# A stretch of constant products on TensorE ahead of the first conditioning product

## The chip, the cores and the metric

The kernel runs on one core of one Trainium2 chip. The metric is the time on the device of one execution, in microseconds (us). The profile is of one execution, taken by the hardware profiler. TensorE appears in it twice: PE is the multiplications, PEld the loads of the stationary operand. DVE is VectorE, ACT is ScalarE, POOL is GpSimd, SP is the engine that issues most transfers.

## What is computed

One step of a one-layer decoder for 256 prompt tokens and 32 sample tokens (8 requests of 4), 288 columns in all, in fp32. Cut to what matters here:

```python
mod = (silu(c) @ w_ada + b_ada)            # conditioning: 9 rows (1 prompt, 8 samples) x 2048 -> 6 x 2048
h = rms(x, g_mix) * (1 + sc_m) + sh_m
proj = h @ w_in                            # 2048 -> 9216: gates, convolution input, u, v, merge gates
...                                        # short convolution, spatial gating, merge
x = x + gt_m * (merged @ w_out)
h2 = rms(x, g_ffn) * (1 + sc_f) + sh_f
x = x + gt_f * ((silu(gate) * up) @ w_ffn_out)   # gate, up = split(h2 @ w_ffn_in)
```

The results are the normalised prompt and sample rows, a new convolution state and normalised rows of v.

## The kernel before, in words

All activations lie transposed: features on the 128 partitions, the 288 tokens along the free dimension. A weight tile is 128x128. It is split into a high and a low part in the format fp32r (ACT casts the high part, line L471; DVE subtracts it, L258 and L478), and `triple` multiplies high by high, high by low and low by high into one PSUM bank: three full-array products, 128x288, lines L239, L242 and L244 (or L241). These are called main products below.

The conditioning product is written another way. `Ada.run` (line L403 of the kernel before) takes as stationary operand `cs`, 32 columns (9 in use) of silu(c), and sends 64, 192 or 512 columns of fp32 weights past it, in four column groups of the array, one for each quarter of a bank:

```python
PE.matmul(acc[32 * j : 32 * j + 32, :w], cs[:, kt, :], self.raw[:, o : o + w],
          ..., tile_position=(0, 32 * j), skip_group_check=True)
```

These products come in visits between main products: a visit is a row of them for j = 0, 1, 2, 3 and several kt. The trace shows two records for each such fp32 product.

TensorE's order is the order in which the code issues, since only that engine is scheduled by hand throughout. The program starts with `warm(19)`, 19 bf16 products of a constant tile `wb` into the bank `idle` (L595), then the first conditioning block `a0[0]`, five more warm products, `a0[1]` with six warm products in its middle, `first_tile` (which makes the first operands, and has eight warm products beside it), and the first main products, stream `w0`:

```python
steps = [Do(lambda: warm(19)), a0[0], Do(lambda: warm(5)), a0[1]]
steps += [Do(first_tile), Do(lambda: warm(6))]
```

Weights arrive from HBM through a ring of seven buffers of 128x2048 fp32 (the tag `raw`, `RAW = 7`), issued by SP in program order: `a0` (2 buffers), `w0`, `a1` (2), `wK`, then the blocks of `wA`. A transfer waits until the ring's buffer is free. PSUM has four banks with the tag `main`, of which `idle` is the first one given out.

Of the kernel before, what the change touches and what calls it, by code (L numbers as in the profile page):

```python
# [8 lines left out]
F32 = mybir.dt.float32  # L9
F32R = mybir.dt.float32r  # L10
# [4 lines left out]
P = 128  # L15
D = 2048
T = 288
# [10 lines left out]
RAW = 7  # L28
# [60 lines left out]
def decoder_kernel(tc, d):  # L89
    nc = tc.nc  # L90
    from contextlib import ExitStack

    with ExitStack() as es:
        def pool(name, bufs=1, **kw):
            return es.enter_context(tc.tile_pool(name=name, bufs=bufs, **kw))

        pc = pool("const")
        pw = pool("wstream")
        pslot = pool("slots", MAIN)
        pkept = pool("kept", KEPT)  # L100
        ptmp = pool("tmp", 5)
        pps = pool("psum", 4, space=bass.MemoryType.PSUM)
        with tc.manual_schedule(engines={nc.tensor.engine}):
            _body(tc, nc, d, pc, pw, pslot, pkept, ptmp, pps)


def _body(tc, nc, d, pc, pw, pslot, pkept, ptmp, pps):
    ids = [0]

    def nm(s):  # L110
        ids[0] += 1
        return f"{s}_{ids[0]}"

    def const(name, shape, dt=F32):
        return pc.tile(shape, dt, tag=name, name=name)
# [12 lines left out]
    def psmain():  # L128
        return pps.tile([P, 512], F32, tag="main", name=nm("pm"), bufs=4)
# [4 lines left out]
    V, A, G, PE, SY = nc.vector, nc.scalar, nc.gpsimd, nc.tensor, nc.sync  # L134
# [26 lines left out]
    cs = const("cs", [P, 16, 32])  # L161
# [205 lines left out]
    class Step:  # L367
        defer = False
        raw = None
# [218 lines left out]
    wb = const("wb", [P, 288], BF16)  # L588
    G.memset(wb, 1.0)
    idle = psmain()  # L590
# [498 lines left out]
        tail.close()  # L1089


    rh1 = h1.__getitem__
    def at(main, plan):
        out, n = [], 0
        for s in main:
            out.append(s)
            if isinstance(s, Blk):
                n += 1
                out += plan.pop(n, [])
        assert not plan  # L1100
        return out
# [71 lines left out]
    n = len(steps)  # L1173
    stream = [s for s in steps if not isinstance(s, Do)]
    pos = {id(s): i for i, s in enumerate(stream)}
    order = list(stream)
# [27 lines left out]
    for s in steps:  # L1204
# [11 lines left out]
        i = pos[id(s)]  # L1216
# [124 lines left out]
```

## Time and profile before

| | |
|---|---|
| time, median of 2 runs | 1594.12 us (1593.86 to 1594.39) |
| profiled execution: its own time | 1594.02 us |
| profiled execution: span of the core | 1592.2 us |
| PE busy | 1582.0 us (99%), 12636 records |
| PEld busy | 1518.1 us (95%) |
| DVE busy, ACT busy | 1016.4 us (64%), 735.9 us (46%) |
| granted TensorE clock, mean | 0.998 |

The span is the profile's stretch from the first to the last instruction; the time of the same execution is 1.8 us longer. The record of a product lasts longer than its step, since products overlap: a step is read from one start to the next.

### The profile page before, as it was taken

How to read it: one execution, taken by the hardware profiler on the slowest of the kernel's cores; microseconds unless marked ns; L12 is line 12 of the kernel's file. 1: busy time of each engine (PE TensorE's matmuls, PEld its weight loads, DVE VectorE, ACT ScalarE, POOL GpSimd, SP SyncE). 2: the span in 40 equal slices, each digit the busy share in tenths (PEclk: the TensorE clock that was granted, in tenths of full speed). 3: DMA queues.
4: the chain of work that ended last, by engine and by line, in shares of the span. 5: the costliest groups of instructions: out<-in, count | busy, mean ns of one | idle time of the engine just before them, and what ended most of it. 6: DMA issues, size and time to landing. Idle time of an engine off the chain costs nothing.

```text
span 1592.2 us, 31593 instructions
## 1 busy us (share of the span) xinstructions
PE 1582.0 (99%) x12636; PEld 1518.1 (95%) x12636; DVE 1016.4 (64%) x2200; ACT 735.9 (46%) x1366; POOL 21.4 (1%) x65
## 2 busy tenths in 40 slices
PE   9999999999999999999999999999999999999997
PEld 8998999998998998999998999999999999999997
DVE  6676788877755667667844555555555555555565
ACT  6633344643444434456643444444444444444464
POOL 0000000000000000011000000000000000000000
PEclk9999999999999999999999999999999999999999
DMA  9887866777778666654766556453564534645341
GB/s 382 332 324 282 324 241 219 282 281 304 287 290 340 270 262 229 250 179 167 271 267 226 216 184 212 160 176 112 168 234 159 173 122 164 229 160 174 113 165 60
DMA packets 59476, 357.88 MB, mean 225 GB/s; under 512 B 6720, under 2 KB 10176, under 8 KB 28608
## 3 DMA queue, kind: packets, MB, share of 16 engines
q1 hardware_dynamic: 59040, 355.73, 60.9%
q8 instruction: 99, 1.62, 0.4%
q14 instruction: 49, 0.40, 0.1%
q10 hardware_dynamic: 288, 0.13, 0.0%
HBM read 352.74 MB, written 3.09 MB: 223 GB/s over the span
## 4 chain that ended last, share of the span: by engine, by line
PE 98%; DMA 1%; DVE 1%; issue 0%; DVEq 0%; ACT 0%; ACTq 0%
PE pm L239 31%; PE pm L244 30%; PE pm L242 30%; PE ada L403 5%; DMA raw<-in_wK 1%; DMA raw<-in_w 0%; DVE st L1070 0%; DMA t<-in_c 0%; DVE q L611 0%; PE px L242 0%; PE px L239 0%; PE px L244 0%; PE px L213 0%; PE px L902 0%; PE px L901 0%; PE px L848 0%
## 5 line engine op out<-in xcount | busy, mean ns | idle before, releaser
L239 PE MATMUL pm<-s,hi 128*128 128x288 f32 (+1 forms) x3750 | 1095.3, 292 | 0.0
L242 PE MATMUL pm<-s,hi 128*128 128x288 f32 (+1 forms) x3750 | 1090.6, 291 | 0.0
L244 PE MATMUL pm<-s,lo 128*128 128x288 f32 (+1 forms) x3738 | 1088.1, 291 | 0.0
L471 ACT CAST hi<-raw 128x512 fp32r<-128x512 f32 (+1 forms) x963 | 585.6, 610 | 770.5 <-PE pm L242 739.1
L478 DVE TENSOR_TENSOR lo<-raw,hi 128x512 fp32r<-128x512 f32 (+1 forms) x849 | 578.8, 683 | 417.8 <-ACT hi L471 405.3
L239 PEld LDWEIGHTS pm<-s,hi 128*128 128x128 f32 x3750 | 702.2, 187 | 15.2 <-issue 12.1
L242 PEld LDWEIGHTS pm<-s,hi 128*128 128x128 f32 x3750 | 702.2, 187 | 0.1
L244 PEld LDWEIGHTS pm<-s,lo 128*128 128x128 f32 x3738 | 699.9, 187 | 0.0
L258 DVE TENSOR_TENSOR lo<-raw,hi 128x512 fp32r<-128x512 f32 x111 | 74.5, 675 | 28.4 <-ACT hi L471 27.6
L403 PE MATMUL ada<-raw,cs 128*32 128x512 f32 (+2 forms) x1152 | 88.2, 453 | 0.0
L403 PEld LDWEIGHTS ada<-raw,cs 128*32 128x32 f32 x1152 | 31.1, 110 | 44.5 <-issue 41.4
L793 DVE TENSOR_TENSOR s<-pm,s 128x288 f32<-128x288 f32 x72 | 32.8, 456 | 18.9 <-PE pm L244 18.6
L311 ACT CAST s<-t 128x288 fp32r<-128x288 f32 (+1 forms) x76 | 32.9, 433 | 19.4 <-DVE t L825 12.5
L313 DVE TENSOR_TENSOR s<-t,s 128x288 fp32r<-128x288 f32 (+1 forms) x76 | 35.0, 461 | 6.5 <-ACT s L311 5.7
L353 DVE SCALAR_TENSOR_TENSOR x<-pm,mod,x 128x256 f32<-128x256 f32 x79 | 37.6, 476 | 0.0
L991 DVE SCALAR_TENSOR_TENSOR t<-t,pm 128x288 f32<-128x288 f32 x42 | 19.1, 455 | 19.6 <-PE pm L244 19.6
L785 DVE TENSOR_TENSOR s<-pm,s 128x288 f32<-128x288 f32 x48 | 21.7, 453 | 9.9 <-PE pm L244 9.2
L352 DVE TENSOR_TENSOR t<-pm,mod 128x32 f32<-128x32 f32 x79 | 15.2, 192 | 16.4 <-PE pm L244 15.9
L776 DVE TENSOR_TENSOR s<-s,rb 128x288 f32<-128x288 f32 x48 | 21.6, 449 | 0.0
L181 ACT ACTIVATE t<-x 128x288 f32<-128x288 f32 x29 | 12.9, 444 | 17.4 <-DVE x L356 17.4
L186 DVE TENSOR_TENSOR acc<-acc,t 128x288 f32<-128x288 f32 x33 | 15.0, 455 | 8.2 <-ACT t L181 8.2
L770 DVE SCALAR_TENSOR_TENSOR s<-pm,s 128x256 f32<-128x256 f32 x36 | 17.3, 481 | 2.7 <-PE pm L244 2.7
(168 smaller groups left out, 478.0 us busy)
## 6 DMA issues: line engine op xcount, KB each, us to landing
raw<-in_fi SPq DMA_DIRECT2D x84, 1024.0 KB, 4.8
raw<-in_a SPq DMA_DIRECT2D x64, 1024.0 KB, 7.3
raw<-in_f SPq DMA_DIRECT2D x64, 704.0 KB, 4.0
raw<-in_wD SPq DMA_DIRECT2D x34, 1024.0 KB, 6.3
raw<-in_aE SPq DMA_DIRECT2D x16, 1024.0 KB, 9.7
raw<-in_wo SPq DMA_DIRECT2D x16, 1024.0 KB, 6.0
raw<-in_wC SPq DMA_DIRECT2D x19, 768.0 KB, 4.2
raw<-in_pa SPq DMA_DIRECT2D x8, 1024.0 KB, 6.4
```

The costliest lines, as they stand in the source:

```text
L239: PE.matmul(out, wh, ah, start=first, stop=False)
L242: end_ = PE.matmul(out, wh, al, start=False, stop=turn and last)
L244: end_ = PE.matmul(out, wl, ah, start=False, stop=last)
L258: lows.pop(0)[1]()
L311: A.copy(hi, a)
L313: V.tensor_tensor(lo, a, hi.bitcast(F32), ALU.subtract)
L353: V.scalar_tensor_tensor(x[:, m, :TP], ps[:, :TP], mod[:, gt0 + m, 0:1], x[:, m, :TP], ALU.mult, ALU.add)
L403: PE.matmul(acc[32 * j : 32 * j + 32, :w], cs[:, kt, :], self.raw[:, o : o + w], start=kt == 0, stop=kt == 15, tile_position=(0, 32 * j), ...
L471: A.copy(hi, self.raw[:, s * 128 : e * 128])
L478: sub()
L785: return V.tensor_tensor(part[m], ps[:, :T], part[m], ALU.add)
L793: V.tensor_tensor(a, ps[:, :T], a, ALU.add)
```

## The change

Before everything that PE does in the program, a function `bench` is called. It fills four tiles of the ring `raw`: `f` (fp32, 0.75) and `r0`, `r1`, `r2` (the same in fp32r). PE then multiplies: 48 bf16 products, 30 main-like products, and 24 kinds of visits. A kind is four times nine main-like products, a product at the border ahead of it (or none), 16 column-group products, a product at the border behind it (or none); and nine main-like products at its end. Twelve kinds vary what stands behind, nine what stands ahead, two the order of the column groups, one the width. Nothing reads the results; they go to the bank `idle` and to the three other banks of the tag `main`.

```diff
+    def bench():
+        f = pw.tile([P, 2048], F32, tag="raw", name=nm("bench"), bufs=RAW)
+        V.memset(f, 0.75)
+        rs = []
+        for i in range(3):
+            r = pw.tile([P, 2048], F32R, tag="raw", name=nm("benchr"), bufs=RAW)
+            A.copy(r, f) if i else V.tensor_copy(r, f)
+            rs.append(r)
+        r0, r1, r2 = rs
+        outs = [idle] + [psmain() for _ in range(3)]
+
+        def main(n):
+            for i in range(n):
+                o = 7 if i % 3 == 0 else 519 if i % 3 == 1 else 7
+                r = r1 if i % 3 == 2 else r0
+                PE.matmul(outs[0][:, :T], r[:, P * (i % 8) : P * (i % 8) + P], r2[:, o : o + T], start=True, stop=True)
+
+        def sets(n, w=512, order=(0, 1, 2, 3)):
+            for i in range(n):
+                for j in order:
+                    PE.matmul(
+                        outs[1][32 * j : 32 * j + 32, :w],
+                        cs[:, i % 16, :],
+                        f[:, 512 * j : 512 * j + w],
+                        start=True,
+                        stop=True,
+                        tile_position=(0, 32 * j),
+                        skip_group_check=True,
+                    )
+
+        def bf(n, m=P, times=1):
+            def g():
+                for _ in range(times):
+                    PE.matmul(outs[2][:m, :n], wb[:, :m], wb[:, :n], start=True, stop=True)
+
+            return g
+
+        def fr(n, m=P):
+            return lambda: PE.matmul(outs[2][:m, :n], r0[:, :m], r2[:, 7 : 7 + n], start=True, stop=True)
+
+        def nat(n, m=P):
+            return lambda: PE.matmul(outs[2][:m, :n], f[:, :m], f[:, :n], start=True, stop=True)
+
+        def none():
+            pass
+
+        def visit(before, after, **k):
+            for _ in range(4):
+                main(9)
+                before()
+                sets(4, **k)
+                after()
+            main(9)
+
+        for i in range(48):
+            PE.matmul(idle[:, :T], wb[:, :P], wb, start=True, stop=True)
+        main(30)
+        for after in (none, bf(2), bf(64), bf(128), bf(T), bf(2, P, 2), bf(2, 32), bf(2, 64), fr(2), fr(64), nat(2), fr(2, 64)):
+            visit(none, after)
+        for before in (bf(2), bf(64), bf(2, 32), bf(2, 64), bf(T), fr(2), fr(2, 32), nat(2, 32), nat(2)):
+            visit(before, none)
+        visit(none, none, order=(3, 2, 1, 0))
+        visit(none, none, order=(0, 2, 1, 3))
+        visit(none, none, w=256)
+
+    bench()
```

A call such as `bf(2, 64)` is a bf16 product of 2 columns with a stationary operand of 64 columns; `fr` is the same in fp32r, `nat` in fp32; without a second number the stationary operand has 128 columns. `bf(2, P, 2)` is two of them.

PE before, around the first conditioning block, which is a0[0] (32 products of 64 columns):

```order
L595 LDWEIGHTS wb
L595 MATMUL pm_100<-wb 128x288
L403 MATMUL ada_163<-raw_103,cs 32x64 x32
L595 LDWEIGHTS wb
L595 MATMUL pm_100<-wb 128x288
```

PE now, at the first border product, in the second kind of visit (`benchr_103` is r0, `benchr_105` is r1, `benchr_107` is r2, `bench_101` is f):

```order
L1107 MATMUL pm_100<-benchr_107,benchr_103 128x288 x2
L1107 MATMUL pm_100<-benchr_107,benchr_105 128x288
L1112 MATMUL pm_109<-bench_101,cs 32x512 x16
L1125 LDWEIGHTS wb
L1125 MATMUL pm_110<-wb 128x2
L1107 MATMUL pm_100<-benchr_107,benchr_103 128x288 x2
L1107 MATMUL pm_100<-benchr_107,benchr_105 128x288
```

PE now reaches its first row of before, the 19 warm products of L595, after 1068 new rows; all that followed them before follows them still.

ACT now, from its start; before, the row behind the ACTIVATE was the cast of w0's first weights (L471):

```order
L138 DMA t_75<-in_c 128x144
L140 DMA cp_77<-in_cpack 128x112
L164 ACT_TABLE_LOAD
L164 ACTIVATE t_87<-t_75 128x144
L1098 CAST benchr_105<-bench_101 128x2048
L1098 CAST benchr_107<-bench_101 128x2048
L471 CAST hi_3033<-raw_2898 128x512
```

Two casts of 2048 columns came in ahead of that cast. On DVE the fill of f and the cast of r0 came in ahead of the two instructions that make cs.

SP now, with what each row waits for; `raw_2904` is a1's first buffer, and the rows and their order are those of before, in which that transfer waited for no engine:

```order
L452 DMA raw_2898<-in_w 128x512 [waits DMAHW2_49]
L385 DMA raw_2904<-in_a 128x1024 [waits DVE_49,DMAHW3_49,PE_49,Activation_49]
L385 DMA raw_2904<-in_a 128x1024 [waits DMAHW4_49]
L385 DMA raw_2907<-in_a 128x1024 [waits DMAHW5_49,PE_49]
L385 DMA raw_2907<-in_a 128x1024 [waits DMAHW6_49]
L155 DMA x<-in_x 128x288 [waits DMAHW7_49]
L454 DMA raw_2911<-in_wK 128x768 [waits DMAHW0_49,PE_49]
```

Since the four tiles of bench take the first four buffers of the ring, a1 and wK now wait for PE to be done with f, r0 and r2, and all later transfers stand behind them.

## The prediction

> **What bounds the kernel now.** I read the head of the page, then the chain of work that ended last, the waits of PE, and the order of time on PE where the new products stand.
>
> ```profile
> span 1592.2 us, 31593 instructions
> PE 1582.0 (99%) x12636; PEld 1518.1 (95%) x12636; DVE 1016.4 (64%) x2200; ACT 735.9 (46%) x1366; POOL 21.4 (1%) x65
> PE 98%; DMA 1%; DVE 1%; issue 0%; DVEq 0%; ACT 0%; ACTq 0%
> ```
>
> PE is busy for 99% of the span and carries 98% of the chain. No other engine is near. Whatever is put on PE is therefore added to the span, save where PE would have stood still or done filler work. PE's only such stretch at the place of the change is the start:
>
> ```profile
> 1.13 4.74 PE L595 MATMUL pm<-wb 128*128 128x288 bf16 x19 [1.13 <-POOL wb L589]
> 5.80 1.24 PE L403 MATMUL ada<-raw,cs 128*32 128x64 f32 x64
> 6.97 0.79 PE L595 MATMUL pm<-wb 128*128 128x288 bf16 x5
> 8.28 0.91 PE L595 MATMUL pm<-wb 128*128 128x288 bf16 x6
> 9.12 0.30 PE L403 MATMUL ada<-raw,cs 128*32 128x64 f32 x5
> ```
>
> The first conditioning block starts at 5.80 us. So I reckon one number, the time at which that block starts in the changed program, and shift all behind it by the difference.
>
> **The start of the new stretch.** The rows also give the price of a bf16 product. The first 19 take 4.74 us, about 0.24 each; six later ones take 0.91 of which the last one's record is 0.29, so 0.91 - 0.29 = 0.62 for five steps, 0.124 each. The slow pace lasts until about 5.9 us: the block at 5.80 still needs 1.24 us where the same 64 records take 1.12 to 1.16 later. The Trainium skill, "TensorE: Matmul & The Clock Gate", section "What's actually happening", says that the clock is at half until one window of about 3.4 us was busy; the two paces in the trace agree with the two rates, though here the slow one lasted some 4.8 us. By 3.4 us the sum below would be about 0.7 us smaller.
>
> The 48 new bf16 products start at 1.13 like the old ones: 20 slow ones to 5.9, then 28 x 0.124 = 3.5, so the main-like products can start at 9.4 us. Their operands must be there by then:
>
> ```profile
> 1.08 0.48 DVE L162 MEMSET cs<- 128x512 f32 x1
> 4.69 0.32 ACT L164 ACTIVATE t<-t 128x144 f32<-128x144 f32 x1 [1.75 <-DMA t<-in_c]
> L471 ACT CAST hi<-raw 128x512 fp32r<-128x512 f32 x892 | 549.8, 618 | 708.0 <-PE pm L242 681.2 <-DMA raw<-in_fi 5.2 <-DVE lo L478 4.7
> L471 ACT CAST hi<-raw 128x384 fp32r<-128x384 f32 x66 | 33.8, 511 | 60.9 <-PE pm L242 57.3 <-DVE gm L700 3.6
> ```
>
> An ACT cast costs 618 ns for 512 columns and 107 ns less for 128 fewer, so 0.62 + 12 x 0.107 = 1.9 us for 2048. Two of them behind the ACTIVATE, which ends at 5.01, are done at 8.8. DVE fills f in about four times 0.48 us, to 3.5, and casts r0 in some 2.4 us (a guess from ACT's 1.9), to 5.9; cs follows within 0.6. The 48 products cover all this by half a microsecond. If that cover were gone, each late microsecond would be one of the result.
>
> **Main-like products.** There are 30 + 24 x (4 x 9 + 9) = 1110, of the shape of the main products.
>
> ```profile
> 880.00:1080.00 200.00, 200.00 (x1545) 200.00 (x1544) 111.81 (x213) 88.06 (x154) 0.00 (x0) 1.00 0.53 181
> ```
>
> In this stretch there is nothing but main products: 1545 records in 200 us plus one record's overhang of 0.29, so 200.29 / 1545 = 0.1296 us each. 1110 x 0.1296 = **143.9 us**.
>
> **Column-group visits.** A visit of before with the very size of the new ones (16 products, 32 records, 512 columns) shows its whole price from main product to main product:
>
> ```profile
> 123.40 0.29 PE L244 MATMUL pm<-s,lo 128*128 128x288 f32 x1
> 123.62 3.64 PE L403 MATMUL ada<-raw,cs 128*32 128x512 f32 x32
> 127.19 0.40 PE L239 MATMUL pm<-s,hi 128*128 128x288 f32 x1
> 127.42 0.29 PE L242 MATMUL pm<-s,hi 128*128 128x288 f32 x1
> ```
>
> From the start at 123.40 to the start at 127.42 are 4.02 us. Two ordinary steps would take 0.26, so the visit adds 3.76. Of this about 0.09 is lost on entry (123.40 to 123.62 instead of 0.13) and about 0.20 to 0.25 on leaving, among it 0.10 by which 127.19 to 127.42 is longer than a step. Since this is a difference of starts, both borders are in it. 23 kinds with 4 visits each: 92 x 3.76 = **345.9 us**.
>
> ```profile
> 43.56 0.29 PE L244 MATMUL pm<-s,lo 128*128 128x298 f32 x1
> 43.78 1.51 PE L403 MATMUL ada<-raw,cs 128*32 128x192 f32 x32
> 45.46 0.31 PE L242 MATMUL pm<-s,hi 128*128 128x298 f32 x1
> ```
>
> The same number of products with 192 columns takes 45.46 - 43.56 = 1.90, less two steps of 0.134 (these are 298 wide), 1.63. Between 1.63 at 192 and 3.76 at 512 columns lies 2.06 at 256; four visits of it are **8.2 us**.
>
> **Border products.** 20 kinds have one, one kind two: 84 products. 52 are bf16, 20 fp32r (12 with 128 stationary columns), 12 fp32 (8 with 128). The trace has small products between main products, none of them in bf16:
>
> ```profile
> 549.15 0.29 PE L244 MATMUL pm<-s,lo 128*128 128x288 f32 x1
> 549.28 0.38 PE L901 MATMUL px<-s,s 128*128 128x128 f32 x2
> 549.95 0.39 PE L902 MATMUL px<-s,s 128*128 128x128 f32 x2
> 550.30 0.29 PE L242 MATMUL pm<-s,hi 128*128 128x288 f32 x1
> 426.85 0.30 PE L244 MATMUL pm<-s,lo 128*128 128x288 f32 x1
> 426.98 0.60 PE L848 MATMUL px<-cp,s 128*128 128x128 f32 x4
> 427.55 0.29 PE L242 MATMUL pm<-s,hi 128*128 128x288 f32 x1
> ```
>
> The four products of L901 and L902 (two records each) lengthen 549.15 to 550.30 by 1.15 - 0.26 = 0.89 us, 0.22 each. The four of L848 lengthen 0.70 by 0.44, 0.11 each. I take 0.22 for an fp32 and 0.11 for an fp32r product with 128 stationary columns, half of it for the narrow ones: 8 x 0.22 + 4 x 0.11 + 12 x 0.11 + 8 x 0.06 = 4.0 us. For a bf16 product the nearest row is the warm one, 0.124 for 288 columns; small ones lie between nothing and that, and I take half, 0.06: 52 x 0.06 = 3.1. Together **7.1 us**.
>
> A page gives a price of its own: the Trainium skill, "TensorE: Matmul & The Clock Gate", section "Wait — 56ns, not 53.3ns?", says that the step never falls below about 25 ns however few columns there are. By that floor the bf16 products would be 1.3 us instead of 3.1, an estimate from the page; no product of the trace stands at that floor.
>
> Both ends for these 84: at best a product does its work inside the loss that a border has anyway, and hides it. the 44 visits with one behind them would save 0.2 each and the 36 with one ahead 0.09 each, some 12 us below nothing. At worst each of them brings a border of its own, 0.33 us (3.76 less eight rounds of 0.43, the step between the load rows below), 84 x 0.33 = 28 us on top of 7.
>
> ```profile
> 124.07 0.13 PEld L403 LDWEIGHTS ada<-raw,cs 128*32 128x32 f32 x4 [0.30 <-issue]
> 124.50 0.13 PEld L403 LDWEIGHTS ada<-raw,cs 128*32 128x32 f32 x4 [0.30 <-issue]
> ```
>
> **The sum.** The new stretch ends at 9.4 + 143.9 + 345.9 + 8.2 + 7.1 = 514.5 us. The 19 warm products stay behind it and now run at the quick pace, 19 x 0.124 = 2.4, then the entry, 0.1: the conditioning block starts at 517.0 instead of 5.80, a shift of 511.2.
>
> Behind that point little can change. PE waited there for 0.16 us at 11.01, 0.35 at 21.03 and 0.20 at 41.30, and the block at 5.80 no longer runs slow (0.1), so at most 0.8 us come back; I count 0.2. What might be lost is the ring: a1, wK and all later transfers now wait for f, r0 and r2.
>
> ```profile
> 6.61 3.13 SPq L385 DMA_DIRECT2D raw<-in_a  x4
> 10.48 8.56 DMA raw<-in_wK
> ```
>
> Before, they were issued from 0.8 us behind the conditioning block's start and wK landed at 19.04, 13.2 behind it. Now f is free at the last visit's end, 1.2 us (nine products) ahead of the warm ones, so a1 is issued some 3.6 us ahead of the block, with a0, w0 and x's first tile long landed and out of the way. The transfers stand about four microseconds better than before, and I cost the wait at nothing. If that cover failed, wK alone needs the 8.56 us of its row.
>
> Span 1592.2 + 511.2 - 0.2 = 2103.2; the execution's own time was 1594.02, 1.8 above its span and 0.1 from the median of the runs. **Forecast 2105 us.**
>
> **Rivals.**
>
> *Each border product brings another drain.* For it: the trace loses 0.33 us on a change between main products and column groups, and a product of another kind or width might count as such a change. Against it: L848's products cost 0.11 with no visible border, and bf16 to column groups and back (7.0 to 9.1 above) shows none beyond the usual. Price up to 28 us: 2133. It decides from about 0.15 us a product. The Trainium skill, "TensorEngine Tiling (Array Packing)", section "Key Properties", states such a rule: a change of tiling mode, not of tile, drains TensorE. The entry and exit above agree with it. By it only products of 64 columns, in a third mode, would pay a further border (12 of them, 1 to 4 us), and the time would be 2106 to 2109, inside my range.
>
> *The border product hides the border.* For it: the 0.10 that the first main product behind a visit loses looks like its load of weights, which nothing covers; a product ahead of it could. Against: a product of 2 columns is too short to cover 0.1. Down to -12 - 7: 2086; likelier -8: 2097.
>
> *The order of the column groups matters.* If 3,2,1,0 or 0,2,1,3 kept the four groups from running side by side, a round would take up to four times as long: 3.4 x 3 = 10 us more a visit, 41 us for one kind, 82 for both: 2146 or 2187. Against: nothing in the rows ties the groups to each other.
>
> *It does nothing.* Nobody reads the products, so they could be taken out when the program is built, or the time might hide under the first transfers. Then 1594, not slower. One mechanism, one price: it decides whether the 1068 rows are in PE's program. They are, and the head start that transfers give is 5.8 us, not 500.
>
> **How the numbers follow.** The forecast with its bounds (2099 to 2113: half or twice the border term, 1% on the main-like products and visits, 0.8 back at the start) 0.74; another drain each 0.12; hiding 0.09; order 0.03; nothing 0.02. The range takes the forecast's own bounds, the likelier half of the drain case and of the hiding case: 2096 to 2122. Slower by over 2% in all cases but the last: 0.98; within 2%, about what a measurement of this kernel can tell from no change, 0.02; faster has no case.
>
> **What would show it.** On the page after: about 510 us more span, PE still at 99%. Main-like steps at 0.1296; bare visits 4.02 from main start to second main start; the group of L1112 with 24 x 4 x 32 = 3072 records; ada's first start near 517. The forecast falls if a kind with a border product stands more than 0.2 us a visit above the bare kind, if a changed order lengthens a visit, or if PE waits for a1 or wK behind 520 us.

## The result, and the profile after

The changed kernel takes 2103.12 us (median of 2 runs, 2103.05 to 2103.19), 1.3194 times the kernel before (95% interval 1.3173 to 1.3215). Forecast were 2105, with 2096 to 2122 as the range. The profiled execution has a span of 2101.4 us against 1592.2, so 509.2 us more.

The head of the page, the chain of work by engine and by line, and the two largest groups of the new stretch (count, busy us, mean ns of a record):

```profile
span 2101.4 us, 40253 instructions
PE 2091.3 (100%) x16962; PEld 1767.8 (84%) x16962; DVE 1020.1 (49%) x2202; ACT 739.4 (35%) x1368; POOL 21.4 (1%) x65
PE 99%; DMA 0%; DVE 0%; ACT 0%; DVEq 0%; issue 0%; SPq 0%
PE pm L239 23%; PE pm L244 23%; PE pm L242 23%; PE pm L1112 16%; PE pm L1107 8%; PE ada L403 4%; DMA x<-in_x 0%; PE pm L1125 0%; DVE st L1070 0%; DMA t<-in_c 0%; ACT benchr L1098 0%; PE px L242 0%; PE px L239 0%; PE pm L1130 0%; PE pm L1133 0%; PE px L244 0%
L1112 PE MATMUL pm<-bench,cs 128*32 128x512 f32 (+1 forms) x3072 | 342.8, 586 | 0.0
L1107 PE MATMUL pm<-benchr,benchr 128*128 128x288 f32 x1110 | 169.8, 300 | 0.2 <-ACT benchr L1098 0.2
```

DVE and ACT have each grown by less than 4 us; PE by 509. The counts are the program's own: 3072 column-group records and 1110 main-like products. The order of time on PE shows the two ends of the new stretch:

```profile
1.13 7.45 PE L1147 MATMUL pm<-wb 128*128 128x288 bf16 x48 [1.13 <-POOL wb L589]
8.80 1.44 PE L1107 MATMUL pm<-benchr,benchr 128*128 128x288 f32 x9 [0.23 <-ACT benchr L1098]
512.18 1.45 PE L1107 MATMUL pm<-benchr,benchr 128*128 128x288 f32 x9
513.47 2.50 PE L595 MATMUL pm<-wb 128*128 128x288 bf16 x19
515.90 1.10 PE L403 MATMUL ada<-raw,cs 128*32 128x64 f32 x64
```

The stretch begins at 8.80 (9.4 was forecast), ends at 513.47, and the first conditioning block starts at 515.90 instead of 5.80, a shift of 510.1 (511.2 was forecast).

The price of a border product is read from one visit to the next. These are the first and the fourth visit of five kinds; between them lie three visits and 27 main-like products:

```profile
14.07 3.64 PE L1112 MATMUL pm<-bench,cs 128*32 128x512 f32 x32
28.91 3.64 PE L1112 MATMUL pm<-bench,cs 128*32 128x512 f32 x32
35.03 3.64 PE L1112 MATMUL pm<-bench,cs 128*32 128x512 f32 x32
38.60 0.18 PE L1125 MATMUL pm<-wb 128*128 128x2 bf16 x1
49.92 3.64 PE L1112 MATMUL pm<-bench,cs 128*32 128x512 f32 x32
161.21 3.64 PE L1112 MATMUL pm<-bench,cs 128*32 128x512 f32 x32
164.78 0.19 PE L1125 MATMUL pm<-wb 128*64 128x2 bf16 x1
176.39 3.64 PE L1112 MATMUL pm<-bench,cs 128*32 128x512 f32 x32
182.62 3.64 PE L1112 MATMUL pm<-bench,cs 128*32 128x512 f32 x32
186.20 0.27 PE L1130 MATMUL pm<-benchr,benchr 128*128 128x2 f32 x1
197.79 3.64 PE L1112 MATMUL pm<-bench,cs 128*32 128x512 f32 x32
374.26 0.17 PE L1130 MATMUL pm<-benchr,benchr 128*128 128x2 f32 x1
374.36 3.64 PE L1112 MATMUL pm<-bench,cs 128*32 128x512 f32 x32
389.18 3.64 PE L1112 MATMUL pm<-bench,cs 128*32 128x512 f32 x32
```

Bare, that is without a border product: (28.91 - 14.07) / 3 = 4.947 us. A bf16 product of 2 columns behind the visit: 4.963, 0.02 more. The same with 64 stationary columns: 5.060, 0.11 more. An fp32r product behind: 5.057, 0.11 more. The same fp32r product ahead of the visit: 4.940, nothing. Read more closely, from the start of the last main-like product ahead of a visit to that of the second one behind it, all kinds give (us above the bare visit, means of four, which agree within 0.006):

| product | behind | ahead |
|---|---|---|
| bf16, 2 columns | 0.02 | 0.02 |
| bf16, 64 / 288 columns | 0.02 / 0.03 | 0.05 / 0.14 |
| bf16, 128 columns; two of 2 columns | 0.02; 0.04 | |
| bf16, 2 columns, 32 stationary columns | 0.00 | 0.00 |
| bf16, 2 columns, 64 stationary columns | 0.12 | 0.12 |
| fp32r, 2 columns | 0.11 | 0.00 |
| fp32r, 64 columns | 0.11 | |
| fp32r, 2 columns, 64 stationary columns | 0.06 | |
| fp32r, 2 columns, 32 stationary columns | | 0.00 |
| fp32, 2 columns | 0.22 | 0.12 |
| fp32, 2 columns, 32 stationary columns | | 0.04 |

The two other orders of the column groups cost nothing; a visit of 256 columns takes 2.06 us, the forecast's value.

### The profile page after: what moved, and what is told of

Its sections match the earlier page's. It is cut to its first block, busy times and chain, and to the rows that moved or that the text cites. A ratio compares the mean times of both kernels' runs of the same rounds, so it can differ in the third digit from the quotient of the medians.

```text
span 2101.4 us, 40253 instructions
## 1 busy us (share of the span) xinstructions
PE 2091.3 (100%) x16962; PEld 1767.8 (84%) x16962; DVE 1020.1 (49%) x2202; ACT 739.4 (35%) x1368; POOL 21.4 (1%) x65
## 4 chain that ended last, share of the span: by engine, by line
PE 99%; DMA 0%; DVE 0%; ACT 0%; DVEq 0%; issue 0%; SPq 0%
PE pm L239 23%; PE pm L244 23%; PE pm L242 23%; PE pm L1112 16%; PE pm L1107 8%; PE ada L403 4%; DMA x<-in_x 0%; PE pm L1125 0%; DVE st L1070 0%; DMA t<-in_c 0%; ACT benchr L1098 0%; PE px L242 0%; PE px L239 0%; PE pm L1130 0%; PE pm L1133 0%; PE px L244 0%
## 5 line engine op out<-in xcount | busy, mean ns | idle before, releaser
L471 ACT CAST hi<-raw 128x512 fp32r<-128x512 f32 (+1 forms) x963 | 585.6, 610 | 763.1 <-PE pm L242 742.7
L1112 PE MATMUL pm<-bench,cs 128*32 128x512 f32 (+1 forms) x3072 | 342.8, 586 | 0.0
L417 DVE STREAM_TRANSPOSE ev<-ada 128x512 f32<-128x512 f32 (+2 forms) x9 | 4.8, 537 | 521.6 <-PE ada L403 521.6
L1112 PEld LDWEIGHTS pm<-bench,cs 128*32 128x32 f32 x3072 | 90.6, 109 | 177.6 <-issue 174.1
L1107 PEld LDWEIGHTS pm<-benchr,benchr 128*128 128x128 f32 x1110 | 148.7, 188 | 44.3 <-issue 43.7
L1107 PE MATMUL pm<-benchr,benchr 128*128 128x288 f32 x1110 | 169.8, 300 | 0.2 <-ACT benchr L1098 0.2
L793 DVE TENSOR_TENSOR s<-pm,s 128x288 f32<-128x288 f32 x72 | 32.8, 456 | 18.9 <-PE pm L244 18.6
```

The costliest lines, as they stand in the source:

```text
L471: A.copy(hi, self.raw[:, s * 128 : e * 128])
L1107: PE.matmul(outs[0][:, :T], r[:, P * (i % 8) : P * (i % 8) + P], r2[:, o : o + T], start=True, stop=True)
L1112: PE.matmul(outs[1][32 * j : 32 * j + 32, :w], cs[:, i % 16, :], f[:, 512 * j : 512 * j + w], start=True, stop=True, tile_position=(0, 32 ...
```

## The experiments

Times of the experiments are to be held against 2103.1 us for the changed kernel; the runs of the kernel before beside them had a median of 1593.8 to 1593.9. The first three experiments are one run each.

### Other kinds of visits

The kinds of the changed kernel give way to these:

```diff
-        def visit(before, after, **k):
+        def visit(before, after, n=4, **k):
...
-                sets(4, **k)
+                sets(n, **k)
...
+        visit(none, none)
+        for before in (fr(2, 64), fr(T), bf(2, 96)):
+            visit(before, none)
+        for after in (fr(T), fr(T, 64), bf(2, 64, 2), bf(2, 32, 2), bf(2, 96)):
+            visit(none, after)
+        for product in (bf(2), bf(T), bf(2, 96), bf(2, 64), bf(2, 64, 2), bf(2, 32), fr(2), fr(2, 64), fr(2, 32), nat(2), nat(2, 32)):
+            visit(none, product, n=0)
+        for n in (1, 2, 8):
+            visit(none, none, n=n)
+        visit(none, none, order=(0, 0, 0, 0))
+        visit(none, none, order=(0, 1, 0, 1))
```

> The stretch of constants has 25 other kinds, so that each price can be read from main product to main product in the profile (bare visit: 4.029 us from start to second start, so 3.77 above two steps of 0.13). Theory A: a border product costs the part of its load and of its stream that nothing covers (about 0.107 us for 128 columns of fp32 or fp32r, 0.054 for 64), and a bf16 or fp32 product with a narrow stationary operand divides the array otherwise, which costs a drain of its own. Theory B: a narrow bf16 operand is just slow to load, 0.12 us each. Above the bare visit, A: ahead, fp32r 2 columns with 64 stationary 0.00, fp32r 288 columns 0.13, bf16 with 96 about 0.05; behind, fp32r 288 columns 0.13, the same with 64 stationary 0.13 - 0.05 = 0.08, two bf16 with 64 about 0.16 (B: 0.24), two bf16 with 32 at most 0.05, bf16 with 96 about 0.05 (B: 0.12). Between main products without a visit, above the steps: bf16 2 columns 0.13, bf16 with 64 and with 32 by A 0.3 or more (two changes), by B 0.23 at most; two with 64 by A 0.35, by B 0.4 or more; fp32r 0.11 whatever the stationary width; fp32 0.22; fp32 with 32 by A 0.33, otherwise 0.14. Visits of 1, 2 and 8 rounds of four products: 1.19, 2.05 and 7.20 (fixed 0.335 and 0.859 a round). All 16 products in one column group: 14.1 if the groups' standing side by side is what makes them cheap, two groups in turn 7.2; if not, 3.77. Time in all about 2023 us.

Measured: 2022.66 us. In the order of time on PE, first and fourth of a kind each: two bf16 products with 64 stationary columns behind a visit; one between main-like products; an fp32r product with 64 there; and the first two visits with all products in one column group:

```profile
141.10 3.64 PE L1112 MATMUL pm<-bench,cs 128*32 128x512 f32 x32
144.67 0.22 PE L1125 MATMUL pm<-wb 128*64 128x2 bf16 x2
156.38 3.64 PE L1112 MATMUL pm<-bench,cs 128*32 128x512 f32 x32
223.79 0.19 PE L1125 MATMUL pm<-wb 128*64 128x2 bf16 x1
228.25 0.19 PE L1125 MATMUL pm<-wb 128*64 128x2 bf16 x1
251.43 0.16 PE L1130 MATMUL pm<-benchr,benchr 128*64 128x2 f32 x1
255.27 0.16 PE L1130 MATMUL pm<-benchr,benchr 128*64 128x2 f32 x1
337.48 13.92 PE L1112 MATMUL pm<-bench,cs 128*32 128x512 f32 x32
352.71 13.92 PE L1112 MATMUL pm<-bench,cs 128*32 128x512 f32 x32
```

Two bf16 products with 64 columns behind a visit: (156.38 - 141.10) / 3 = 5.093, 0.15 above bare: the second one adds 0.03, not another 0.12. One between main-like products: (228.25 - 223.79) / 3 = 1.487 against 9 x 0.13 = 1.17, so 0.32. With 32 stationary columns, the visit's own width, such a product costs 0.00 at a visit (the table above) and 0.30 between main-like products. The price sits on the change to such a product and back, not on the product: theory A stands, B (0.24 and at most 0.23) falls. An fp32r product in the same place costs (255.27 - 251.43) / 3 - 1.17 = 0.11, with 128, 64 or 32 stationary columns alike: in fp32r a narrow operand shows no price for a change of division. With all products in one group a visit recurs every 15.23 us instead of 4.95: the four groups' standing side by side is worth 10.3 us a visit, the price that the rival on the order had.

The other kinds, above the bare visit or the plain steps: ahead, fp32r with 64 stationary 0.00, fp32r of 288 columns 0.13, bf16 with 96 stationary 0.00 (0.05 was expected); behind, fp32r of 288 columns 0.13, the same with 64 stationary 0.08, two bf16 with 32 0.01, bf16 with 96 0.04; between main-like products, bf16 of 2 columns 0.13, of 288 0.14, with 96 stationary 0.11, two with 64 0.35, with 32 0.30, fp32 0.22, fp32 with 32 0.35. Visits of 1, 2 and 8 rounds: 1.20, 2.05 and 7.20. Two groups in turn: 7.19.

### The visits without their border products

```diff
-            visit(none, after)
+            visit(none, none)
...
-            visit(before, none)
+            visit(none, none)
```

> The 84 border products are left out, everything else of the change stays. If the prices read from the profile add up (12 prices behind, 9 ahead, four visits each: 4.94 us), the time falls from 2103.1 to 2098.2 us. If the products hide in the borders, it stays at 2103.1; if each had cost the 7.1 us that the sum of the prediction had for all, 2096.0; with a drain for each of them (28 us) 2070.

Measured: 2098.15 us, 4.97 less than the changed kernel. From the first main-like product (8.68 us here, 8.80 there) to the end of the span it is 2096.4 - 8.68 = 2087.7 against 2092.6, 4.9 less. The single prices add up.

### The main-like products alone

```diff
             for _ in range(4):
                 main(9)
-                before()
-                sets(4, **k)
-                after()
             main(9)
```

> The visits and the border products are left out, the 1110 main-like products, the 48 and the fills stay. By the sum: 92 x 3.769 + 4 x 2.062 + 4.94 = 359.9 us less, 1743.2 us. If the visits had slowed the main-like products around them beyond their own borders, more is saved (below 1742); if the transfers at the start had hidden behind the visits, less.

Measured: 1743.82 us, 0.6 above the sum. Its first main-like product starts at 9.64 instead of 8.80 us, 0.84 later, because its 48 bf16 products took 8.77 us instead of 7.45 (see the last section); without that the visits and border products are worth 360.2 us where 359.9 were added up. They do not slow their neighbours beyond their borders, and no transfer hid behind them.

### The border price in the kernel's own work

The kernel before, with this behind each row of conditioning blocks:

```diff
         s.run()
+        if isinstance(s, Ada) and not (i + 1 < len(stream) and isinstance(stream[i + 1], Ada)):
+            PE.matmul(psmisc()[:64, :2], wb[:, :64], wb[:, :2], start=True, stop=True)
```

> The kernel before, without the new stretch, with one bf16 product of 2 columns and 64 stationary columns behind each of 22 rows of conditioning blocks, its result unread. If the price of such a border (0.120 us in the new stretch) holds in the kernel's own work, the time is 1594.1 + 22 x 0.12 = 1596.7 us, and each visit in the profile is 0.12 longer. If the kernel has slack there, 1594.1; if the extra PSUM tiles make PE wait, more than 1597.

Measured: 1596.41 us, 1.0015 times the kernel before (1.0006 to 1.0025), 2.5 us more beside 1593.87. The visit of four blocks that the prediction quotes, in this run:

```profile
124.31 0.29 PE L244 MATMUL pm<-s,lo 128*128 128x288 f32 x1
124.53 3.64 PE L403 MATMUL ada<-raw,cs 128*32 128x512 f32 x32
128.10 0.19 PE L1229 MATMUL px<-wb 128*64 128x2 bf16 x1
128.22 0.39 PE L239 MATMUL pm<-s,hi 128*128 128x288 f32 x1
128.45 0.29 PE L242 MATMUL pm<-s,hi 128*128 128x288 f32 x1
```

From 124.31 to 128.45 are 4.14 us, 0.12 more than the 4.02 of before. A price measured between constants is the price in the kernel's work, and hardly any slack takes it up: 2.5 us of the 2.6 expected show.

### Without the 19 bf16 products behind the stretch

```diff
-    steps = [Do(lambda: warm(19)), a0[0], Do(lambda: warm(5)), a0[1]]
+    steps = [a0[0], Do(lambda: warm(5)), a0[1]]
```

> The changed kernel without the 19 bf16 products (L595) that stand between the new stretch and the first conditioning block. By the sum they cost 19 x 0.123 = 2.4 us there, since PE has nothing to wait for: 2100.7 us. Rival, the ring: a1, wK and all behind them are issued only when the new stretch lets go of its buffers, 3.5 us ahead of the conditioning block, and now only 1.1 us ahead; if those transfers end late, PE waits and up to all of the gain is lost: 2103.1.

Measured: 2101.42 us (2100.82 to 2101.80), 1.7 less than the changed kernel. The two ends of the stretch again:

```profile
1.13 8.83 PE L1147 MATMUL pm<-wb 128*128 128x288 bf16 x48 [1.13 <-POOL wb L589]
9.70 0.52 PE L1107 MATMUL pm<-benchr,benchr 128*128 128x288 f32 x2
513.05 1.45 PE L1107 MATMUL pm<-benchr,benchr 128*128 128x288 f32 x9
514.43 0.77 PE L403 MATMUL ada<-raw,cs 128*32 128x64 f32 x40
```

In this execution the 48 products needed 8.83 us instead of 7.45, and the stretch began 0.9 us later, at 9.70. From there to the end of the span are 2099.9 - 9.70 = 2090.2 us, against 2101.4 - 8.80 = 2092.6: 2.4 less, the whole price of the 19. The ring's rival falls: with a1 issued 1.2 us ahead of the conditioning block nothing waits for it.

### Without the 48 bf16 products at the start

```diff
-        for i in range(48):
-            PE.matmul(idle[:, :T], wb[:, :P], wb, start=True, stop=True)
```

> The changed kernel without the 48 bf16 products at the start of the new stretch. By the prediction they cost nothing as long as the casts of r1 and r2 end only at 8.8 us: the first main-like product would still start at 8.8. But then PE begins at the slow clock, 0.24 us a step for some 3.4 to 4.8 us, 14 to 20 products with 0.11 more each: 1.6 to 2.2 us longer, 2104.7 to 2105.3 us. Rival: the 48 are a plain cost (7.4 us) and the time falls towards 2096; or the clock does not matter, 2103.1.

Measured: 2106.13 us (2105.53 to 2106.21), 1.3213 times the kernel before (1.3193 to 1.3233), 3.0 more than the changed kernel. The busy time of PE, PEld, DVE, ACT and POOL in the first 4.4 us of the stretch, with the count of records in brackets and, ahead of the last two columns, the granted clock; then PE's first products, and a row from behind the conditioning block:

```profile
8.98:13.40 4.42, 4.42 (x18) 4.42 (x19) 0.00 (x0) 0.62 (x1) 0.00 (x0) 1.00 0.49 187
8.98 4.63 PE L1107 MATMUL pm<-benchr,benchr 128*128 128x288 f32 x18 [8.98 <-ACT benchr L1098]
524.25 0.43 PE L525 MATMUL pm<-s,hi 128*128 128x298 f32 x2 [0.54 <-issue]
```

PE waits for the casts until 8.98 and then runs 18 products at about 0.24 us a step, though the granted clock reads 1.00. That and the later start bring the conditioning block 2.2 us later (518.10), as expected. Behind that block another 0.7 us is lost (2104.3 - 518.10 = 1586.2 against 1585.5), at a stop ahead of 524.25 that the profile puts down to nothing and that no other trace has there. It is not explained, and it is why the time of this execution lies above the expected 2105.3; whether the executions without a profile have it is not shown. The rival of the plain cost falls, and so does the one by which the clock does not matter.

## Why the prediction was right, point by point

- **PE carries the chain, so the new products add in full.** Right: 509.2 us of span, PE 99% of the chain. The rival in which nothing happens had nothing for it.
- **Main-like products and visits, 498.0 us.** The stretch took 513.47 - 8.80 = 504.7, of which 4.9 are border products: 499.7, 1.7 above the sum. The visits, 3.77 where 3.76 was read, make 0.9 of it. The other steps, 0.1305 on average where 0.1296 was read, make 0.8; those just behind a visit are the longer ones.
- **Border products, 7.1 us.** They cost 4.9, and both terms were too large: bf16 cost 2.3 where 3.1 was taken, fp32 and fp32r 2.6 where 4.0 was. One price of 0.06 for every bf16 product was wrong in its parts: 0.02 for most, 0.12 for the eight with 64 stationary columns, 0.14 for the four of 288 columns ahead of a visit. For fp32r the prediction took 0.11 or half of it on either side, where a product ahead of a visit costs nothing. The loads of the fp32r products of 2 columns show why; the first two rows are behind a visit, the third is ahead of one:

```profile
186.19 0.19 PEld L1130 LDWEIGHTS pm<-benchr,benchr 128*128 128x128 f32 x1 [0.84 <-issue]
186.30 0.70 PEld L1107 LDWEIGHTS pm<-benchr,benchr 128*128 128x128 f32 x5
374.13 0.19 PEld L1130 LDWEIGHTS pm<-benchr,benchr 128*128 128x128 f32 x1
```

Behind a visit the load starts together with its product (186.19 and 186.20), and the next load follows only 0.11 us later. Ahead of a visit the load starts at 374.13, together with the last main-like product, and the visit begins at 374.36, 0.22 later as in the bare kind.

- **A drain for every product (a rival)** fell; its narrow form held for bf16. The Trainium skill, "TensorEngine Tiling (Array Packing)", section "Key Properties", has the drain only on a change of tiling mode. The trace agrees for bf16: 64 stationary columns cost 0.12 at a visit and 0.32 between main products, 32 columns, the visit's own mode, 0.00 and 0.30. Of the 12 products that were to pay by that rule, the eight in bf16 did, 1.0 us together; the four in fp32r cost 0.06 each, and fp32r pays for no width between main products (0.11 with all three).
- **A border product that hides the border (a rival).** No kind came out below the bare visit, so the price of 8 to 19 us less fell. Its mechanism shows all the same: a bf16 product of 288 columns costs 0.14 ahead of a visit and 0.03 behind one, where the main-like product's load is uncovered anyway and can run beside its columns. An fp32r product of 288 columns gains nothing from that (0.13 on either side), since behind a visit its own load is uncovered. This reading of the loads is an argument; the 0.08 with 64 stationary columns, half the load, fits it.
- **The order (a rival)** had the right price, 10 us a visit, and the wrong condition: what counts is how many different groups stand in a round, not their order.
- **The floor of a step.** The Trainium skill, "TensorE: Matmul & The Clock Gate", section "Wait — 56ns, not 53.3ns?", gives it as about 25 ns, however few the columns. No bf16 product here starts that soon behind another: two of 2 columns start 0.04 to 0.05 us apart, though the second lengthens the whole by 0.02 to 0.03 only. By that floor the bf16 products would have cost 1.3 us, an estimate from that page; they cost 2.3.
- **A sign of being wrong** came true: the fp32 product of 2 columns behind a visit stands 0.22 above the bare kind, over the 0.2 that was named. The prediction's own price for it was 0.22, so the sign was set too low and does not speak against the mechanism.
- **The start, 9.4 us.** It was 8.80. The prediction took the later of two bounds, the 48 products (9.4) and the casts (8.8). Here the slow pace ended at 4.0 us and not at 5.9, so the 48 were through by 1.13 + 7.45 = 8.58, and PE waited 0.23 us for ACT's second cast, which ended at 8.75. The cover of half a microsecond was gone, and the cast set the start. The pace had no error bar and needed one (below).
- **The ring, at no cost; 0.2 us back.** No cost, and 0.9 came back. Of the two rows that follow, the first is before, the second after. Before, the cast waited until wK landed at 19.04, though its row names DVE; now wK landed at about 521.6 (issued at 514.92, 6.7 us to landing), 3.7 us ahead of the cast. So the wait of 0.35 at 21.03 is no longer listed, worth 0.4; the quicker first block gave the 0.1 forecast for it. Another 0.2 is luck: PE stops near 110.3 in the trace of before for no reason that the profile shows, and in no other trace. The waits of 0.16 and 0.20 stayed.

```profile
19.12 0.51 ACT L471 CAST hi<-raw 128x384 fp32r<-128x384 f32 x1 [3.61 <-DVE gm L700]
525.32 0.56 ACT L471 CAST hi<-raw 128x384 fp32r<-128x384 f32 x1
```

The four errors, -0.6 at the start, +1.7, -2.2 and -0.7, make the -1.8 us between forecast span and span. That the whole is off by less than its largest term is in part luck: the +1.7 offsets most of the -2.2.

## What to carry to other kernels

On an engine that is never idle, a change of starts between two like neighbours prices a piece of work with all its borders, and such prices added up to within 1% here. Where a small product stands at a change of array division (from the full array to column groups, or back) decides what it costs. An fp32r product of 2 columns costs its load, 0.11 us, behind the change, and nothing ahead of it, where the stream of the product ahead covers the load. A bf16 product of 288 columns costs 0.14 ahead and 0.03 behind. Keep a narrow bf16 product in the division that its neighbours use.

## What the runs showed that I had not expected

The half pace at the start lasts a different time in each execution. In the five profiled ones with the 48 products, these took 7.45, 7.60, 7.61, 8.77 and 8.83 us, with 12 to 24 steps of 0.24 us from the first product at 1.13 us, so 2.9 to 5.7 us of it; the granted clock in the profile read 1.00 all the while. In the two long ones the first main-like product follows the 48 directly, at 9.64 and 9.70 us. In the three short ones it starts at 8.68, 8.80 and 8.86, 0.05 us behind the end of ACT's second cast: there the casts set it. Differences below 1 us between two versions with such a start are to be read from a point behind it.
